# Stick-breaking attention: running products against differences of successive values, in place of a second sigmoid and a product per key

## The chip, the core and the metric

The kernel runs on one core of a Trainium2 chip. The metric is the device time of one execution in microseconds, the median of several. The engines are TensorE (PE, with its weight loads shown as PEld), VectorE (DVE), ScalarE (ACT), GpSimd (POOL) and SyncE (SP), which issues the DMAs of this kernel. Each engine works through its own instructions in order and waits on semaphores.

## What is computed

A decoder trunk of two layers over 1024 tokens of width 1024, in float32. The even layer has two kinds of softmax attention, the odd one stick-breaking attention with 16 heads of width 64; each is followed by a SwiGLU layer, and a norm closes. The change touches stick-breaking attention alone:

```python
z = jnp.einsum('bhqd,bhkd->bhqk', q_c, k).astype(jnp.float32) * scale
log_rest = jnp.where(strict, jax.nn.log_sigmoid(-z), 0.0)
suffix = lax.cumsum(log_rest, axis=3, reverse=True) - log_rest
a = jnp.where(strict, jnp.exp(jax.nn.log_sigmoid(z) + suffix), 0.0)
return jnp.einsum('bhqk,bhkd->bhqd', a.astype(v.dtype), v)
```

`strict` keeps the keys ahead of the query. With m the sigmoid of −z (1 where masked) and R(j) the product of m over the keys from j on, the weight of key j is (1 − m(j)) R(j+1), which is R(j+1) − R(j). A sum over keys of these differences times v(j) is therefore the sum of R(j) (v(j−1) − v(j)) plus the last value of the block, as R behind the last key is 1 and the value ahead of the first key counts as 0.

## The kernel before, in words

`sb_attention` works on eight chunks `i` of two heads `hh` each. A chunk's attention is cut into units `unit(i, hh, c)`, `c` from 0 to 3, each with two blocks of 128 query rows (`qb`) against `nk = (qb + 1) * 128` keys. A unit has three stages. `s0` loads the queries twice over the partitions (`qs`). `s1` makes the scores of both blocks on TensorE into one of two PSUM tiles (`b..s`, `ps_s`), two sigmoids on ScalarE (`m` of −z, `e` of z), a scan from the right on VectorE that turns `m` into running products, and a multiply on VectorE, of `e` by `m` shifted by one key, which gives the weights:

```python
nc.scalar.activation(like(m, sv, 0, nk), sv, AF.Sigmoid, scale=-1.0)
nc.scalar.activation(like(e, sv, 0, nk), sv, AF.Sigmoid)
...
nc.vector.tensor_tensor(e[:, :nk - 1], e[:, :nk - 1], m[:, 1:nk], op=ALU.mult)
```

`s2` turns the weights by transposes on TensorE into PSUM (`b..t`), splits them there into a rounded high half (`ph`, ScalarE) and the rest (`pl`, VectorE), and multiplies both by V, whose 128 columns hold the high and the low half of a head's 64 values (`b..o`, one PSUM tile, `ps_o`). ScalarE copies the lower 64 rows out and VectorE adds them to the upper ones (`ot`), and the result is stored to DRAM (`o2T_d`). TensorE can start the next unit's `b..o` only behind that sum.

The projections are generators that `run_segments` runs between the units as fill: `qk_chunk(i)` makes a chunk's queries and keys (`sqo`, `qc`, `kc`, `ks`) in 8 steps, `v_chunk(i)` makes V for two chunks (`svo`, `sv`) in 8 steps, one for each tile of 128 tokens. V of the first two chunks is made alone, ahead of any unit; V of chunks 2 and 3, 4 and 5, 6 and 7 beside the units of chunks 1, 3 and 5. In the last two chunks the fill is the output projection (`obo`), whose weights (`obw`) are loaded then.

The order on each engine is not written out by hand: a scheduler at build time lays the instructions out by its own estimate of when each can run, and each engine then keeps to that order.

Of the kernel before, what the change touches and what calls it, by code (L numbers as in the profile page):

```python
# [11 lines left out]
F32 = mybir.dt.float32  # L12
# [3 lines left out]
ALU = mybir.AluOpType  # L16
# [23 lines left out]
def trunk(ctx: ExitStack, tc: tile.TileContext, x, norm_mix, norm_ffn, norm_final,  # L40
# [19 lines left out]
    def ps_t(name):  # L60
        return ps.tile([128, 512], F32, name=name, tag="t", bufs=3)
# [86 lines left out]
    def alt(pf, i):  # L148
        return pf[i % len(pf)] if pf else None
# [908 lines left out]

    def sb_attention(h, op):
        w_in = odd_w_in[0]  # L1060
        with pool("sv", 2) as sv_, pool("sq", 2) as sq, pool("sa", 2) as sa:
            vbox, qbox = {}, {}

            def v_chunk(i, pf=None):
                w = load_w(w_in, 0, KT, [(2 * D + i * 256, 256)], f"sv{i}", nc.gpsimd)
                vs = [sv_.tile([128, NT, 2, 128], F32R, name=f"sv{i}{j}", tag="V", bufs=3) for j in range(2)]
                vbox[2 * i], vbox[2 * i + 1] = vs
                for tt in range(NT):
                    o = proj_tok(h, tt, w, 256, f"svo{i}{tt}", alt(pf, tt))
                    for j in range(2):  # L1070
                        src = o[:, j * 128:(j + 1) * 128].rearrange("p (h d) -> p h d", d=64)
                        nc.scalar.copy(vs[j][:, tt, :, 0:64], src)  # L1072
                        nc.vector.tensor_tensor(vs[j][:, tt, :, 64:128], src,  # L1073
                                                vs[j][:, tt, :, 0:64].bitcast(F32), op=ALU.subtract)
                    yield

            def qk_chunk(i, pf=None, by_half=False):
# [31 lines left out]
            def unit(i, hh, c):  # L1109
# [10 lines left out]
                def s1():  # L1120
                    qst = pts.pop()
                    kst = qbox[i][1][hh]
                    for qb in (2 * c, 2 * c + 1):
                        nk = (qb + 1) * 128
                        s = ps_s(f"{nm}s{qb}")
                        qsl = slice(qb % 2 * 128, (qb % 2 + 1) * 128)
                        sv = qk(s, (qst[:, 0, qsl], qst[:, 1, qsl]), kst, 0, nk, [(nk - 128, m_strict)])
                        e = sa.tile([128, (c + 1) * 256], F32, name=f"{nm}e{qb}", tag=f"E{c}", bufs=2)
                        m = sa.tile([128, (c + 1) * 256], F32, name=f"{nm}m{qb}", tag=f"M{c}", bufs=1)
                        nc.scalar.activation(like(m, sv, 0, nk), sv, AF.Sigmoid, scale=-1.0)  # L1130
                        nc.scalar.activation(like(e, sv, 0, nk), sv, AF.Sigmoid)
                        mr = m[:, :nk][:, ::-1]
                        nc.vector.tensor_tensor_scan(mr, mr, zc[:, :1].to_broadcast([128, nk]), 1.0,
                                                     op0=ALU.mult, op1=ALU.add)
                        nc.vector.tensor_tensor(e[:, :nk - 1], e[:, :nk - 1], m[:, 1:nk], op=ALU.mult)
                        pts.append(e)

                def s2():
                    v = vbox[i]
                    o = ps_o(f"{nm}o")[:, :256]  # L1140
# [28 lines left out]
                    nc.scalar.copy(tmp[0:64], o[64:128, :])  # L1169
                    nc.vector.tensor_tensor(tmp[pr], o[0:64, :], tmp[0:64], op=ALU.add)  # L1170
                    if i == 7:
# [14 lines left out]
            for i in range(8):  # L1186
# [3 lines left out]
                elif i % 2 == 1:  # L1190
                    segs.append((units, [v_chunk((i + 1) // 2), qk_chunk(i + 1)], 16, 2))
                elif i == 6:
# [77 lines left out]
```

## Time and profile before

| | |
|---|---|
| runs | 2796.96 us median of 3 (2796.86 to 2797.99) |
| profiled execution | 2809.49 us, span of its instructions 2807.7 us |
| busy share of the span | TensorE 95%, its weight loads 82%, VectorE 67%, ScalarE 44%, GpSimd 19% |
| stick-breaking layer | from about 1464 to 2110 us of the span |

The span goes from the first to the last instruction. A wait is idle time of an engine right ahead of an instruction, with the instruction of another engine that ended it. Names are those of the program: `b613o` is the output tile of unit i = 6, hh = 1, c = 3, and `<-` stands between what is written and what is read. The granted clock (PEclk) is 1.00 at TensorE's 2.4 GHz and 0.50 at 1.2 GHz. Shares of idle time in a stretch are its length less the engine's busy time.

### The profile page before, as it was taken

Reading aid. Unit: us, or ns where it says so; the run is one execution under the profiler, and the core shown is the slowest. Engines: PE = TensorE matmul, PEld = TensorE weight load, DVE = VectorE, ACT = ScalarE, POOL = GpSimd, SP = SyncE. Lnnn points to the kernel's source line nnn. Section 1 sums busy time; section 2 is a strip of 40 time slices with the busy share of each in tenths; the row PEclk is TensorE's granted clock in tenths of the full one; section 3 lists DMA queues with packets and bytes.
Section 4 is the critical chain, followed back from the end, with each engine's and each line's share of the span. In section 5 each row is a group of like instructions: output and inputs, shape, how many; then the busy total and the mean of one; then the engine's idle time right before and its main releaser. Section 6 shows DMA issues by size and latency. Waiting matters only on the chain.

```text
span 2807.7 us, 42453 instructions
## 1 busy us (share of the span) xinstructions
PE 2668.3 (95%) x15596; PEld 2307.8 (82%) x15596; DVE 1880.9 (67%) x3266; ACT 1244.9 (44%) x2603; POOL 525.6 (19%) x637
## 2 busy tenths in 40 slices
PE   8999999999979999999999999999887999999998
PEld 7889888898967888888887888787786788888887
DVE  7467667556586666657554767877848657665755
ACT  4366666544353333334443545554425333333433
POOL 3465655444120000000022020211102000000000
PEclk9999999999989999999999999999998999999999
DMA  5100000013445555577643233324434545556754
GB/s 157 32 23 7 23 21 22 23 45 95 123 175 176 150 163 166 159 224 240 198 162 87 59 83 69 94 68 110 124 102 166 174 153 167 160 158 212 256 186 141
DMA packets 327904, 347.70 MB, mean 124 GB/s; under 512 B 24560, under 2 KB 280208, under 8 KB 327696
## 3 DMA queue, kind: packets, MB, share of 16 engines
q1 hardware_dynamic: 327696, 344.98, 40.5%
q8 instruction: 124, 2.03, 0.3%
q14 instruction: 84, 0.69, 0.1%
HBM read 223.79 MB, written 95.94 MB: 114 GB/s over the span
## 4 chain that ended last, share of the span: by engine, by line
PE 69%; DVE 13%; DMA 9%; issue 4%; ACT 4%; POOL 2%; SPq 1%; DVEq 0%; POOLq 0%; ACTq 0%
PE f0o L128 2%; PE f0o L126 2%; PE f0o L127 2%; PE f1o L128 2%; PE f1o L126 2%; PE f1o L127 2%; PE sqo L126 2%; PE sqo L127 2%; PE sqo L128 2%; DMA f1t<-in_ffn_w_down_dram 1%; PE svo L126 1%; PE svo L128 1%; PE svo L127 1%; DMA t_d<-f1t 1%; PE oao L127 1%
## 5 line engine op out<-in xcount | busy, mean ns | idle before, releaser
L113 POOL TENSOR_SCALAR sv0h<-sv0r 128x1024 fp32r<-128x1024 f32 x2 | 2.1, 1057 | 598.9 <-DVE f0c L1043 595.2
L167 POOL TENSOR_TENSOR nf0r<-nf0v,mhalf 128x1 f32<-128x1 f32 x1 | 0.6, 553 | 600.6 <-DVE nf0v L165 600.6
L208 PEld LDWEIGHTS <-ident_b 128*128 128x128 bf16 x352 | 34.2, 97 | 48.2 <-issue 35.7
L1043 DVE TENSOR_TENSOR f1c<-f1o,f1c 128x512 f32<-128x512 f32 x56 | 36.0, 687 | 30.2 <-PE f1o L128 30.1
L1043 DVE TENSOR_TENSOR f0c<-f0o,f0c 128x512 f32<-128x512 f32 x56 | 36.0, 684 | 18.8 <-PE f0o L128 18.8
L951 DVE TENSOR_TENSOR f1t<-f1t 128x256 f32<-128x256 f32 x22 | 9.4, 425 | 51.0 <-DMA f1t<-in_ffn_w_down_dram 51.0
L951 DVE TENSOR_TENSOR f0t<-f0t 128x256 f32<-128x256 f32 x22 | 9.4, 425 | 50.2 <-DMA f0t<-in_ffn_w_down_dram 50.2
L1072 ACT CAST sv<-svo 128x128 fp32r<-128x128 f32 x64 | 17.0, 268 | 48.7 <-PE svo L128 36.3
L1073 DVE TENSOR_TENSOR sv<-svo,sv 128x128 fp32r<-128x128 f32 x64 | 18.2, 286 | 30.0 <-ACT sv L1072 29.8
L702 POOL TENSOR_SCALAR obh<-obr 128x1024 fp32r<-128x1024 f32 (+1 forms) x8 | 12.1, 1530 | 88.8 <-DMA obr<-o2T_d 45.0
L1102 DVE TENSOR_TENSOR kc<-sqo,kc 128x512 fp32r<-128x512 f32 x16 | 11.0, 689 | 23.4 <-ACT kc L1101 23.3
L735 DVE TENSOR_TENSOR xr<-obo,xr 128x256 f32<-128x256 f32 x32 | 13.3, 419 | 18.1 <-PE obo L128 17.9
L735 DVE TENSOR_TENSOR xr<-oao,xr 128x256 f32<-128x256 f32 x32 | 13.3, 419 | 16.6 <-PE oao L128 16.4
L1097 DVE SCALAR_TENSOR_TENSOR qc<-sqo,qc 128x512 fp32r<-128x512 f32 x16 | 11.0, 687 | 18.5 <-ACT qc L1096 18.5
L1101 ACT CAST kc<-sqo 128x512 fp32r<-128x512 f32 x16 | 9.4, 588 | 30.3 <-PE sqo L128 30.3
L126 PE MATMUL cgo<-cgh,hah 128*128 128x280 f32 x64 | 19.7, 309 | 1.7 <-ACT hah L192 1.7
L128 PE MATMUL cgo<-cgh,hal 128*128 128x280 f32 x64 | 20.0, 313 | 0.0
L127 PE MATMUL kso<-ksl,hah 128*128 128x256 f32 x64 | 18.9, 296 | 1.2 <-POOL ksl L115 1.2
L127 PE MATMUL cgo<-cgl,hah 128*128 128x280 f32 x64 | 19.5, 305 | 0.0
L126 PE MATMUL kso<-ksh,hah 128*128 128x256 f32 x64 | 18.6, 294 | 0.9 <-ACT gates L400 0.9
L126 PE MATMUL q0o<-q0h,hah 128*128 128x256 f32 x64 | 19.1, 301 | 0.0
L126 PE MATMUL dk1o<-dk1h,hah 128*128 128x256 f32 x64 | 18.8, 294 | 0.1
(9997 smaller groups left out, 11121.6 us busy)
## 6 DMA issues: line engine op xcount, KB each, us to landing
f0t<-in_ffn_w_down_dram SPq DMA_DIRECT2D x44, 256.0 KB, 3.9
t_d<-f0t SPq DMA_DIRECT2D x22, 512.0 KB, 3.0
f1t<-in_ffn_w_down_dram SPq DMA_DIRECT2D x44, 256.0 KB, 3.9
t_d<-f1t SPq DMA_DIRECT2D x22, 512.0 KB, 2.9
f0dr<-t_d SPq DMA_DIRECT2D x20, 512.0 KB, 4.9
f1dr<-t_d SPq DMA_DIRECT2D x20, 512.0 KB, 5.1
x_d<-xr SPq DMA_DIRECT2D x64, 128.0 KB, 2.3
ks<-kc SPq DMA_DIRECT2D x64, 128.0 KB, 2.3
```

Source lines behind the costliest of these rows:

```text
L126: nc.tensor.matmul(o, a[0], b[0], start=start, stop=False, skip_group_check=onto)
L127: nc.tensor.matmul(o, a[0], b[1], start=False, stop=False, skip_group_check=onto)
L128: nc.tensor.matmul(o, a[1], b[0], start=False, stop=stop, skip_group_check=onto)
L208: nc.tensor.matmul(s[:, b, mo:mo + 128], ident_b, m, start=False, stop=i == len(here) - 1)
L702: nc.gpsimd.tensor_scalar(hs, raw, 1.0, 1.0, op0=ALU.mult, op1=ALU.mult)
L735: nc.vector.tensor_tensor(xr, o[:, :256], xr, op=ALU.add)
L951: nc.vector.tensor_tensor(b11, b12, b11, op=ALU.subtract)
L1043: nc.vector.tensor_tensor(cv, o, cv, op=ALU.add)
L1072: nc.scalar.copy(vs[j][:, tt, :, 0:64], src)
L1073: nc.vector.tensor_tensor(vs[j][:, tt, :, 64:128], src, vs[j][:, tt, :, 0:64].bitcast(F32), op=ALU.subtract)
L1097: nc.vector.scalar_tensor_tensor(lo, o, SCALE, hi.bitcast(F32), op0=ALU.mult, op1=ALU.subtract)
L1102: nc.vector.tensor_tensor(kc[:, 1, :], o, kc[:, 0, :].bitcast(F32), op=ALU.subtract)
```

## The change

The second sigmoid and the multiply go, and with them the tiles `e`. The transposes read the running products, `m`, which now has two buffers (three for the larger `c`) in place of one. V holds differences: `v_chunk` copies a projected tile to SBUF (`vf`), shifts it by one token by DMAs (rows 0 to 126 into rows 1 to 127 of `d`, called `vb` in the pool; row 127 into row 0 of the next tile's), and subtracts; the split into high and low halves then reads the difference from SBUF in place of PSUM. Row 127 of each tile, the last value of each block of keys, also goes by DMA into a row of `rows`, which four small transposes turn into `ends`, and `s2` adds the right column of `ends` in the sum that makes `ot`. That makes a ninth step of `v_chunk`, and the fill count of its segments goes from 16 to 17.

```diff
             def v_chunk(i, pf=None):
...
                 vs = [sv_.tile([128, NT, 2, 128], F32R, name=f"sv{i}{j}", tag="V", bufs=3) for j in range(2)]
-                vbox[2 * i], vbox[2 * i + 1] = vs
-                for tt in range(NT):
-                    o = proj_tok(h, tt, w, 256, f"svo{i}{tt}", alt(pf, tt))
+                ends = sv_.tile([64, 4, NT], F32, name=f"se{i}", tag="ends", bufs=2)
+                rows = sv_.tile([NT, 256], F32, name=f"sr{i}", tag="rows", bufs=1)
+                vbox[2 * i], vbox[2 * i + 1] = [(vs[j], ends[:, 2 * j:2 * j + 2, :]) for j in range(2)]
+                before = [sv_.tile([128, 256], F32, name=f"sb{i}0", tag="vb", bufs=5)]
+                nc.vector.memset(before[0][0:1, :], 0.0)
+                steps = []
+
+                def split(tt):
+                    d, vf = steps[tt]
+                    nc.vector.tensor_tensor(d, d, vf, op=ALU.subtract)
                     for j in range(2):
-                        src = o[:, j * 128:(j + 1) * 128].rearrange("p (h d) -> p h d", d=64)
+                        src = d[:, j * 128:(j + 1) * 128].rearrange("p (h d) -> p h d", d=64)
                         nc.scalar.copy(vs[j][:, tt, :, 0:64], src)
                         nc.vector.tensor_tensor(vs[j][:, tt, :, 64:128], src,
                                                 vs[j][:, tt, :, 0:64].bitcast(F32), op=ALU.subtract)
+
+                for tt in range(NT):
+                    o = proj_tok(h, tt, w, 256, f"svo{i}{tt}", alt(pf, tt))
+                    vf = sv_.tile([128, 256], F32, name=f"sf{i}{tt}", tag="vf", bufs=4)
+                    nc.scalar.copy(vf, o[:, :256])
+                    d = before.pop()
+                    nc.sync.dma_start(d[1:128, :], vf[0:127, :])
+                    nc.sync.dma_start(rows[tt:tt + 1, :], vf[127:128, :])
+                    if tt < NT - 1:
+                        before.append(sv_.tile([128, 256], F32, name=f"sb{i}{tt + 1}", tag="vb", bufs=5))
+                        nc.sync.dma_start(before[0][0:1, :], vf[127:128, :])
+                    steps.append((d, vf))
+                    if tt > 1:
+                        split(tt - 2)
                     yield
+                split(NT - 2)
+                split(NT - 1)
+                t = ps_t(f"set{i}")
+                for j in range(4):
+                    nc.tensor.transpose(t[:64, j * NT:(j + 1) * NT], rows[:, j * 64:(j + 1) * 64], ident[:NT, :NT])
+                nc.scalar.copy(ends, t[:64, :4 * NT].rearrange("p (j t) -> p j t", j=4))
+                yield
...
-                        e = sa.tile([128, (c + 1) * 256], F32, name=f"{nm}e{qb}", tag=f"E{c}", bufs=2)
-                        m = sa.tile([128, (c + 1) * 256], F32, name=f"{nm}m{qb}", tag=f"M{c}", bufs=1)
+                        m = sa.tile([128, (c + 1) * 256], F32, name=f"{nm}m{qb}", tag=f"M{c}", bufs=3 if c > 1 else 2)
                         nc.scalar.activation(like(m, sv, 0, nk), sv, AF.Sigmoid, scale=-1.0)
-                        nc.scalar.activation(like(e, sv, 0, nk), sv, AF.Sigmoid)
                         mr = m[:, :nk][:, ::-1]
                         nc.vector.tensor_tensor_scan(mr, mr, zc[:, :1].to_broadcast([128, nk]), 1.0,
                                                      op0=ALU.mult, op1=ALU.add)
-                        nc.vector.tensor_tensor(e[:, :nk - 1], e[:, :nk - 1], m[:, 1:nk], op=ALU.mult)
-                        pts.append(e)
+                        pts.append(m)
...
-                    v = vbox[i]
+                    v, ends = vbox[i]
...
-                    nc.vector.tensor_tensor(tmp[pr], o[0:64, :], tmp[0:64], op=ALU.add)
+                    for k in range(2):
+                        cs = slice(k * 128, (k + 1) * 128)
+                        nc.vector.scalar_tensor_tensor(tmp[pr, cs], o[0:64, cs], ends[:, hh, 2 * c + k:2 * c + k + 1],
+                                                       tmp[0:64, cs], op0=ALU.add, op1=ALU.add)
...
-                    segs.append((units, [v_chunk((i + 1) // 2), qk_chunk(i + 1)], 16, 2))
+                    segs.append((units, [v_chunk((i + 1) // 2), qk_chunk(i + 1)], 17, 2))
```

The order on the engines moves with it. First VectorE where unit b013 is finished and the units of chunk 1 begin, before (L1133 is the scan, L1135 the multiply, L1156 makes `pl`, L1170 makes `ot`):

```order
L1133 SCALAR_TENSOR_TENSOR b102m_18217<-b102m_18217,zc 128x640
L1133 SCALAR_TENSOR_TENSOR b101m_18083<-b101m_18083,zc 128x512
L1135 TENSOR_TENSOR b102e_18216<-b102e_18216,b102m_18217 128x639
L1135 TENSOR_TENSOR b101e_18082<-b101e_18082,b101m_18083 128x511
L1156 TENSOR_TENSOR b013pl_18015<-b013t_18009,b013ph_18014 128x512
L1156 TENSOR_TENSOR b013pl_18028<-b013t_18022,b013ph_18027 128x512
L1133 SCALAR_TENSOR_TENSOR b102m_18229<-b102m_18229,zc 128x768
L1133 SCALAR_TENSOR_TENSOR b103m_18362<-b103m_18362,zc 128x896
L1170 TENSOR_TENSOR b012ot<-b012o,b012ot 64x256
L1135 TENSOR_TENSOR b102e_18228<-b102e_18228,b102m_18229 128x767
L1156 TENSOR_TENSOR b013pl_18041<-b013t_18035,b013ph_18040 128x512
```

and the same place of the changed kernel (L1161 is the scan, L1183 makes `pl`, L1199 makes `ot`; `se` is `ends`):

```order
L1161 SCALAR_TENSOR_TENSOR b101m_18097<-b101m_18097,zc 128x512
L1183 TENSOR_TENSOR b013pl_18032<-b013t_18026,b013ph_18031 128x512
L1183 TENSOR_TENSOR b013pl_18045<-b013t_18039,b013ph_18044 128x512
L1199 SCALAR_TENSOR_TENSOR b012ot<-b012o,se_17041,b012ot 64x128 x2
L1183 TENSOR_TENSOR b013pl_18058<-b013t_18052,b013ph_18057 128x512
L1161 SCALAR_TENSOR_TENSOR b102m_18244<-b102m_18244,zc 128x640
L1161 SCALAR_TENSOR_TENSOR b102m_18253<-b102m_18253,zc 128x768
```

The multiplies are gone from between, the sum `ot` of unit b012 is two instructions, and the scans of block b102 stand behind the first three `pl` of b013 instead of among them.

Second, VectorE a little later, where V of chunks 2 and 3 is made, in the changed kernel (`sb` is the shifted tile `d`, `sf` the copied one; L1078 is the new subtraction, L1082 the split's):

```order
L1078 TENSOR_TENSOR sb10_18135<-sb10_18135,sf10_18162 128x256
L1199 SCALAR_TENSOR_TENSOR b013ot_18078<-b013o_18025,se0_17041,b013ot_18078 64x128 x2
L1082 TENSOR_TENSOR sv10_18131<-sb10_18135,sv10_18131 128x2x64
L1082 TENSOR_TENSOR sv11_18132<-sb10_18135,sv11_18132 128x2x64
L1078 TENSOR_TENSOR sb11_18166<-sb11_18166,sf11_18193 128x256
L1199 SCALAR_TENSOR_TENSOR b100ot_18114<-b100o_18100,se0_17041,b100ot_18114 64x128 x2
L1082 TENSOR_TENSOR sv10_18131<-sb11_18166,sv10_18131 128x2x64
L1082 TENSOR_TENSOR sv11_18132<-sb11_18166,sv11_18132 128x2x64
L1183 TENSOR_TENSOR b101pl0_18263<-b101t0_18257,b101ph0_18262 128x512
L1183 TENSOR_TENSOR b101pl2_18275<-b101t2_18270,b101ph2_18274 128x256
```

Before, only the split's instructions (L1073), which read the projection's PSUM tile, stood in these places; now a subtraction that waits for a DMA stands directly ahead of `ot` of units b013 and b100 and ahead of `pl` of b101.

Third, TensorE behind the last matmul of that V, in the changed kernel (L205 and L208 make scores and add the mask, L1103 are the four transposes of `rows`, L1177 the transposes of a unit):

```order
L128 MATMUL svo17_18498<-sv1h4_18127,hcl11_16744 128x256
L205 MATMUL b112s4_18763<-ks11_17528,b112qs_18672 128x320 x4
L208 LDWEIGHTS ident_b_76
L208 MATMUL b112s4_18763<-m_strict_85,ident_b_76 128x128
L205 MATMUL b112s5_18772<-ks11_17528,b112qs_18672 128x384 x4
...
L205 MATMUL b113s6_18848<-ks11_17528,b113qs_18760 128x448 x4
...
L205 MATMUL b113s7_18857<-ks11_17528,b113qs_18760 128x512 x4
...
L1103 MATMUL set1_18542<-ident_69,sr1_18134 64x8 x4
L1177 MATMUL b103t0_18566<-ident_69,b103m6_18405 128x128
```

The transposes of `rows` are new there; four blocks of scores stand between them and the projection in this chunk, two in the next two chunks of V, and 31 projection matmuls in the first.

## Rows read from the trace of the kernel before

**Rows 1.** The page's first part: busy us (share of the span) xinstructions.

```profile
PE 2668.3 (95%) x15596; PEld 2307.8 (82%) x15596; DVE 1880.9 (67%) x3266; ACT 1244.9 (44%) x2603; POOL 525.6 (19%) x637
```

**Rows 2.** Busy time by stretch of the stick-breaking layer, whole core.

```profile
core 0: us, PE busy (x) PEld busy (x) DVE busy (x) ACT busy (x) POOL busy (x), PEclk, DMA share, GB/s
1520.00:1600.00 80.00, 70.20 (x422) 59.47 (x420) 68.38 (x87) 46.34 (x99) 9.22 (x4) 0.94 0.33 74
1600.00:1680.00 80.00, 77.10 (x488) 67.36 (x488) 52.63 (x74) 38.25 (x84) 15.64 (x9) 1.00 0.29 70
1680.00:1760.00 80.00, 75.72 (x528) 67.99 (x528) 64.53 (x96) 44.72 (x104) 14.46 (x8) 0.98 0.31 72
1760.00:1840.00 80.00, 76.48 (x444) 64.22 (x443) 61.34 (x81) 43.74 (x89) 14.56 (x8) 1.00 0.38 91
1840.00:1920.00 80.00, 76.55 (x513) 68.40 (x512) 58.16 (x83) 40.97 (x95) 11.37 (x7) 0.98 0.28 67
1920.00:2000.00 80.00, 70.90 (x440) 60.51 (x439) 71.54 (x93) 43.72 (x90) 13.54 (x9) 0.96 0.48 123
2000.00:2060.00 60.00, 52.70 (x395) 50.25 (x396) 48.46 (x67) 22.34 (x48) 8.37 (x6) 0.91 0.38 112
```

**Rows 3.** TensorE's waits from 1520 to 2060 us, longest first: total, times, longest.

```profile
PE b613o L1162 <- DVE b612ot L1170: 2.9, 1, 2.9
PE b602t L1150 <- DVE kc L1102: 2.7, 1, 2.7
PE b002o L1162 <- DVE b001ot L1170: 2.7, 1, 2.7
PE b213t L1150 <- DVE b212pl L1156: 1.7, 1, 1.7
```

**Rows 4.** Busy time right behind the wait of `b002o`; columns as in rows 2.

```profile
1540.10:1546.90 6.80, 5.96 (x25) 5.29 (x25) 6.28 (x12) 2.06 (x6) 0.00 (x0) 0.50 0.56 132
```

**Rows 5.** Busy time of line 1135, the multiply, in the whole layer.

```profile
1464.00:2130.00 666.00, 103.60 (x128) 0.97 0.37 96
```

**Rows 6.** Busy time of line 1131, the second sigmoid, whole layer.

```profile
1464.00:2130.00 666.00, 83.90 (x128) 0.97 0.37 96
```

**Rows 7.** Groups by line and shape: busy us, mean ns | idle before.

```profile
L1130 ACT ACTIVATE b113m<-b113s 128x1024 f32<-128x1024 f32 x1 | 1.0, 1028 | 2.4 <-DVE b113e L1135 2.4
L1133 DVE TENSOR_TENSOR_SCAN b013m<-b013m,zc 128x1024 f32<-128x1024 f32 x1 | 2.3, 2292 | 1.2 <-ACT b013m L1130 1.2
L1135 DVE TENSOR_TENSOR b013e<-b013e,b013m 128x1023 f32<-128x1023 f32 x1 | 1.2, 1225 | 0.1
L1073 DVE TENSOR_TENSOR sv<-svo,sv 128x128 fp32r<-128x128 f32 x64 | 18.2, 286 | 30.0 <-ACT sv L1072 29.8
L735 DVE TENSOR_TENSOR xr<-obo,xr 128x256 f32<-128x256 f32 x32 | 13.3, 419 | 18.1 <-PE obo L128 17.9
```

**Rows 8.** Tile `b102ot`: duration ns min/median/max, first and last start us.

```profile
L1169 ACT COPY b102ot<-b102o x1: 375/375/375, 1619.4 to 1619.4; 64x256 f32<-64x256 f32 x1
```

**Rows 9.** Groups of TensorE by line and shape, columns as in rows 7.

```profile
L1150 PE MATMUL b703t<-ident,b703e 128*128 128x128 f32 x15 | 2.3, 273 | 0.0
L205 PE MATMUL b103s<-ks,b103qs 128*128 128x512 f32 x4 | 1.2, 419 | 0.0
```

**Rows 10.** Line 1105, DMA issues: duration ns min/median/max, first, last start.

```profile
L1105 SPq DMA_DIRECT2D ks<-kc x64: 461/572/944, 1506.6 to 1978.9; - x64
```

**Rows 11.** ScalarE in order of time, V projected alone: start, us, instruction.

```profile
1483.79 0.27 ACT L1072 CAST sv<-svo 128x128 fp32r<-128x128 f32 x1 [1.99 <-PE svo L128]
1486.67 0.27 ACT L1072 CAST sv<-svo 128x128 fp32r<-128x128 f32 x1 [1.99 <-PE svo L128]
```

**Rows 12.** The page's sixth part: DMA issues, KB each, us to landing.

```profile
ks<-kc SPq DMA_DIRECT2D x64, 128.0 KB, 2.3
```

## Prediction

> **What bounds the kernel now.** I read the page's busy times first, then busy time by stretch, then TensorE's waits, then the groups of the two operations that go. The reader is to see in the first that TensorE is busy for 95% of the span and VectorE for 67% [rows 1]: work taken from VectorE counts only where TensorE waits for it. The change touches the stick-breaking layer alone, which runs from 1464 to about 2110 us of the span; ahead of it the order of every engine stays as it was, and in the second SwiGLU layer behind it the same work only changes places by some rows.
>
> In that layer the stretches [rows 2] show two things side by side. TensorE is idle for 80 − 70.20 = 9.80 us of the first 80 us, then 2.90, 4.28, 3.52, 3.45 and 9.10 us, and 7.30 us of the last 60: together 40.35 us. VectorE's share in the same stretches is 85, 66, 81, 77, 73, 89 and 81%. The two stretches with most idle time are those with the fullest VectorE; at 66 to 77% the idle time is 2.9 to 3.5 us. The waits say the same of single places [rows 3]: the long ones of TensorE end on VectorE, on the small sum of a unit's outputs (`ot`), on the low halves (`pl`), on the keys' low halves (`kc`). These are not the removed multiply itself, but instructions that stand behind it on VectorE's queue. The multiply sits in front of them 128 times.
>
> The third cost is the clock. The granted clock over these stretches is 0.94, 1.00, 0.98, 1.00, 0.98, 0.96 and 0.91 [rows 2]; with 0.06 × 80 + 0.02 × 80 + 0.02 × 80 + 0.04 × 80 + 0.09 × 60 that is 16.6 us lost. Right after the 2.7 us wait before `b002o` the clock stood at 0.50 (1.2 instead of 2.4 GHz) for a whole 6.8 us, in which TensorE was busy 5.96 us [rows 3, 4]. So at most 40 + 17 = 57 us can be won here, if nothing of TensorE's own work changes.
>
> **What goes.** 128 multiplies on VectorE, 103.60 us in sum, 0.81 us each [rows 5]; 128 sigmoids on ScalarE, 83.90 us, 0.66 us each [rows 6]. The path of a block shortens, too: for the last row block of a head, scores to transposes was sigmoid 1.03 us, a second sigmoid of the same width, scan 2.29, multiply 1.23 [rows 7]; the scan does not read the second sigmoid, so the path loses the multiply, 1.2 us, and, where ScalarE is behind, up to 1 us more. A score bank is free one sigmoid earlier. And the single buffer of `m` made ScalarE wait for the multiply of the block before (2.4 us ahead of `b113m` [rows 7]); with two or three buffers that wait goes.
>
> **What comes.** On VectorE: 32 subtractions of 128x256 at 0.42 us (a sum of that size [rows 7]) = 13.4 us; the 64 subtractions into the low half of V stay at 0.29 [rows 7], reading SBUF instead of PSUM; the unit's sum of 64x256 becomes two of 64x128, at 0.29 each by the row of that width, against 0.41: 64 × 0.17 = 11 us. Net on VectorE 104 − 24 = 80 us less, 15 points of its share over the 540 us. On ScalarE 32 copies of 0.38 us [rows 8] = 12 us against 84. ScalarE is busy for 37 to 58% of these stretches [rows 2] and stays hidden.
>
> On TensorE: 16 transposes of eight rows. The nearest row has 15 transposes in 2.3 us [rows 9]: 0.15 each, 2.5 us; bounds 0 and 2.5, I take 2.
>
> On SyncE: 23 more DMAs for each of four chunks, each about 0.57 us to issue [rows 10], 13 us a chunk. Three of them per token tile are 1.7 us against the 2.88 us that a tile's projection takes [rows 11], so the queue keeps up where the tiles come back to back. Behind them stand the loads of `qs`, issued a unit ahead, the stores of `o2T_d`, which the output projection reads much later, and the weights' loads.
>
> **The two new waits.** (a) The transposes of `rows` need the last tile's row 127: copy 0.38, issue of the shift 0.57, then 2.3 us to landing by the DMA of `ks` [rows 8, 10, 12], 3.2 us after the projection's last matmul. In chunk 0, 31 projection matmuls stand between, which hides it; in chunk 1 four blocks of scores; in chunks 2 and 3 only two, of four matmuls and about 1.2 us each [rows 9], 2.4 us. Everything on TensorE is queued behind. Bounds 0 and 3 × 3.2 = 10 us; I take 3 × 1 = 3 us. (b) VectorE's subtraction waits for the shifted rows, up to 3.2 us behind the copy, and in the new order it stands directly ahead of `ot` and `pl` of the running unit (second piece of the order). But the next tile's projection covers 2.88 us of it on TensorE [rows 11]. Bounds: 0, and 24 tiles × 3.2 = 77 us if nothing were covered; nearest is the uncovered 0.3 us, 24 × 0.3 = 7 us, of which some falls where VectorE has slack: I take 3. The eight tiles of chunk 0 run before any unit and delay nobody.
>
> **The sum.** What idle time is left I read off the same table: VectorE's shares fall by 15 points to about 70, 51, 66, 62, 58, 74 and 66%. A stretch of before with such a share had 2.90 us idle at 66%, 3.45 at 73%, and none below is shown, so I give 3.2, 2.9, 2.9, 2.9, 2.9, 3.5 and, for 60 us, 2.2: 20.5 us. That is 20 us less. Stretches with up to 3.5 us idle lost 0 to 1.6 us to the clock, 0.5 on average; seven of them lose 3.7 instead of 16.6. Of the 13 us between, 88% (5.96 of 6.8 [rows 4]) were on busy time, and I take 10. Total 30 us won, 2 + 3 + 3 = 8 lost: 22 us less. The profiled execution took 2809.49 us (span 2807.7), 12.5 above the median of the runs, 2796.96. So span 2785, and median 2797 − 22 = 2775 us.
>
> **Rivals.**
> *More comes back.* If nearly every wait on VectorE vanishes and the clock stays up, 57 − 8 = 49 us: 2748. For it: nearly all long waits of TensorE end on VectorE. Against it: the stretch with VectorE at 66% still had 2.90 us idle [rows 2].
> *Nothing comes back.* TensorE's order was laid out again for the shorter chain. If transposes now stand closer behind their scores, a wait returns with the same length, as the order gives away what the chain saved: idle stays at 40, the clock too, and 2 + 3 remain to be paid, so 2797 + 5 = 2802; with half of it, 2797 − 15 + 8 = 2790. The pieces of the order speak for it a little: fewer rows stand between a scan and what reads it. Against it: VectorE's load falls by 80 us whatever the order. The Trainium skill, "Perfetto Trace Analysis", section "Identifying the Most-Contended Engine", says to improve the engine with the highest occupancy first and to judge TensorE by its weight loads. By that TensorE is the engine (its loads fill 438 of the 540 us of the seven stretches), the change adds to it, and the time would be 2802 as well; the same page's next section says to go after what fills the gaps of that engine, which is the forecast's side. The trace has both: high occupancy and gaps that end on VectorE [rows 2, 3].
> *Slower.* The shifted rows come late. If VectorE stood for half of the 3.2 us at each of the 24 tiles of chunks 1 to 3 with TensorE waiting behind, 24 × 1.6 = 38 us, in place of the 3 taken: 2797 − 22 + 35 = 2810. It turns the gain into a loss from about 1.1 us per tile on. For it: an in-order VectorE, three DMAs in one in-order queue, copies on a ScalarE that itself waits for casts. Against it: 2.88 us of cover per tile, and the buffers (five and four) let copies run ahead.
>
> **Chances.** The likeliest case, gain of 10 to 42 us: 0.68. More: 0.08. Nothing or nearly nothing (2790 to 2802): 0.15. Slower by the rows: 0.09. A measurement of this kernel can tell 0.2%, 5.6 us, from no change: faster means below 2791.4, slower above 2802.6. From the cases: faster 0.68 + 0.08 + 0.05 = 0.81, same 0.10, slower 0.09. Leaving out a tenth on each side, the range is 2750 to 2797; the likeliest case alone spans 2755 to 2787.
>
> **What the profile of the changed kernel would show.** Right: VectorE's busy time in the seven stretches near 345 us instead of 425, TensorE in them idle for some 20 us with the clock at 0.98 or better, the layer ending some 20 us earlier, the copy of `ends` hardly waited for. Wrong: TensorE's waits as long as before but ending on scans or sigmoids (nothing comes back); waits of `ot`, `pl` or casts behind line 1078 that end on a DMA, or TensorE standing more than 3 us ahead of line 1103 (slower). Idle time well below 15 us would mean that 2.9 us was no floor, and the time lies under 2760.

## The result, and the profile after

The changed kernel takes 2944.65 us (median; 2933.94 to 2946.79) against 2797.47 us for the kernel before in the same measurement: ratio 1.0513, 95% interval 1.0482 to 1.0543. The forecast of 2775 us was a gain; the change is a loss, and the time lies 170 us above the forecast. The page's first part of the changed kernel, to be set beside [rows 1]:

```profile
span 2944.3 us, 42511 instructions
...
PE 2702.4 (92%) x15612; PEld 2337.5 (79%) x15612; DVE 1810.4 (61%) x3238; ACT 1183.9 (40%) x2511; POOL 514.6 (17%) x637
```

VectorE lost 70 us of work and ScalarE 61, as the change is meant to do. TensorE's share nevertheless fell from 95 to 92%: it waits. Where, a table by stretch shows. The stretches are cut where TensorE begins a stage: the lone projection of the first V; then alternately chunks of units beside which no V is made (2nd, 4th, 6th row) and chunks beside which it is (3rd, 5th, 7th); the last row is the rest of the layer's units. Changed kernel, columns as in [rows 2]:

```profile
1461.40:1548.90 87.50, 58.66 (x311) 51.48 (x309) 17.72 (x39) 12.00 (x36) 11.02 (x7) 0.79 0.19 52
1548.90:1595.40 46.50, 43.59 (x251) 35.89 (x251) 33.20 (x42) 21.75 (x45) 7.08 (x5) 1.00 0.40 91
1595.40:1720.50 125.10, 90.03 (x527) 79.72 (x526) 49.95 (x84) 34.10 (x85) 14.21 (x9) 0.81 0.25 58
1720.50:1772.20 51.70, 49.00 (x299) 41.30 (x298) 38.60 (x51) 24.46 (x54) 6.11 (x4) 1.00 0.39 91
1772.20:1895.10 122.90, 86.31 (x526) 76.33 (x524) 48.81 (x87) 33.77 (x86) 14.47 (x9) 0.83 0.24 57
1895.10:1946.90 51.80, 48.86 (x300) 41.25 (x298) 38.69 (x51) 24.40 (x54) 6.11 (x5) 1.00 0.39 91
1946.90:2072.10 125.20, 88.06 (x526) 77.77 (x524) 48.46 (x86) 33.71 (x86) 13.65 (x8) 0.84 0.22 52
2072.10:2237.70 165.60, 152.91 (x1081) 140.40 (x1079) 109.93 (x168) 56.59 (x124) 20.54 (x17) 0.96 0.46 126
sum 776.30, PE 617.43 PEld 544.14 DVE 385.37 ACT 240.78 POOL 93.17; mean PE 77.18 PEld 68.02 DVE 48.17 ACT 30.10 POOL 11.65
```

The same stages of the kernel before, cut in the same way:

```profile
1464.50:1511.10 46.60, 46.60 (x307) 42.87 (x306) 12.53 (x29) 10.20 (x27) 10.85 (x7) 1.00 0.27 74
1511.10:1565.50 54.40, 48.35 (x251) 39.75 (x251) 43.13 (x50) 30.68 (x60) 8.15 (x4) 0.91 0.36 83
1565.50:1652.80 87.30, 79.06 (x521) 69.88 (x520) 58.18 (x85) 39.75 (x92) 17.09 (x9) 0.98 0.28 68
...
1704.90:1785.20 80.30, 77.35 (x523) 69.38 (x521) 57.35 (x83) 41.24 (x94) 13.94 (x8) 0.98 0.32 77
...
1838.20:1918.40 80.20, 77.25 (x522) 69.28 (x520) 57.37 (x83) 41.19 (x94) 13.17 (x7) 0.98 0.30 71
...
sum 630.60, PE 581.11 PEld 514.00 DVE 453.11 ACT 300.33 POOL 103.10; mean PE 72.64 PEld 64.25 DVE 56.64 ACT 37.54 POOL 12.89
```

The four stages that make V grew by 40.9, 37.8, 42.6 and 45.0 us, 166 together. All others shrank, by 20.6 us together (776.30 − 630.60 = 145.7 in sum). The traced execution of the kernel before lay 12.5 us above its median, so the 20.6 us are rather too many. So the change does two things at once: the units are quicker, and the making of V is much slower. In the slow stages TensorE is idle for 29 to 37 us and the granted clock is 0.79 to 0.84 (a mean of its two levels, 1.00 and 0.50), so that its busy time grew too (90.03 for 79.06 us with nearly the same work, 527 matmuls for 521). Of the 166 us, 123.5 are idle time and 42.8 busy time.

TensorE's waits in the changed kernel, longest first, in the place of [rows 3]:

```profile
PE svo L126 <- ACT sf L1088: 33.2, 5, 8.1
PE sqo L126 <- ACT sf L1088: 13.7, 2, 7.4
PE set L1103 <- DMA sr<-sf: 11.0, 1, 11.0
PE set L1103 <- DMA sv3r<-in_odd_w_in_dram: 10.7, 1, 10.7
PE b502t L1177 <- ACT sf L1088: 6.9, 1, 6.9
PE b102t L1177 <- DVE sv L1082: 6.4, 1, 6.4
```

The longest no longer end on `ot`, `pl` or `kc`. Three of these six end on ScalarE's copy of a projected tile (`sf`, line 1088), and two stand ahead of the transposes of the end rows (`set`, line 1103). These transposes do not read `sv3r`, so the releaser named in the fourth line is probably not the true one. The groups by line, columns as in [rows 7], say what stands behind these waits:

```profile
L1078 DVE TENSOR_TENSOR sb<-sb,sf 128x256 f32<-128x256 f32 x32 | 15.0, 468 | 190.2 <-DMA sb<-sf 182.1
...
L1081 ACT CAST sv<-sb 128x128 fp32r<-128x128 f32 x64 | 16.3, 296 | 204.0 <-DVE sb L1078 204.0
...
L1103 PE MATMUL set<-ident,sr 8*64 8x8 f32 x16 | 1.4, 195 | 28.0 <-DMA sr<-sf 11.0
```

The new subtraction waits 182 us in all for the shifted rows, 5.7 us for each of 32; ScalarE's casts wait 204 us for the subtraction. One turn of this, in order of time, while V is projected alone:

```profile
1464.98 0.37 ACT L1088 COPY sf<-svo 128x256 f32<-128x256 f32 x1 [1.14 <-PE svo L128]
...
1465.38 0.78 SPq L1090 DMA_DIRECT2D sb<-sf  x1
...
1473.45 0.43 DVE L1078 TENSOR_TENSOR sb<-sb,sf 128x256 f32<-128x256 f32 x1 [6.25 <-DMA sb<-sf]
...
1473.91 0.50 ACT L1081 CAST sv<-sb 128x128 fp32r<-128x128 f32 x2 [7.43 <-DVE sb L1078]
...
1474.32 0.37 ACT L1088 COPY sf<-svo 128x256 f32<-128x256 f32 x1
...
1474.71 0.63 SPq L1090 DMA_DIRECT2D sb<-sf  x1
```

The shift is issued 0.40 us after the copy began; the subtraction starts 8.07 us later; the cast 0.46 behind that; and the *next* tile's copy 0.41 behind the cast, because it stands behind it on ScalarE. That is 9.34 us per tile, where [rows 11] have 2.88. During the transfer the DMA engines are nearly empty (columns as in [rows 2]; the last three are clock, DMA share and GB/s):

```profile
1467.80:1472.60 4.80, 4.80 (x43) 4.80 (x42) 0.00 (x0) 0.00 (x0) 0.00 (x0) 1.00 0.07 23
```

0.07 of 16 engines is about one engine, and 127 KB at 23 GB/s take 5.7 us. The theory to be tested is that the 127 rows go out through one DMA engine (A). Its rivals are the single-row transfers and SyncE's issue (B); the new subtraction's place in the order as such, whatever the transfer takes (C); and that the units' part gave nothing either (D). The scheduler at build time is called the planner from here on; it lays the order out anew for every edit, so for each run the order has to be looked at, too. Below, "behind the cast" counts the copies that stand on ScalarE behind a cast of the tile just before, of the 28 that have a tile before them; in the changed kernel it is 21.

### The profile page after: what moved, and what is told of

The parts are those of the page before. It is cut to its first block, busy times and chain, and to the rows that moved or that the text cites. A ratio compares the mean times of both kernels' runs of the same rounds, so it can differ in the third digit from the quotient of the medians.

```text
span 2944.3 us, 42511 instructions
## 1 busy us (share of the span) xinstructions
PE 2702.4 (92%) x15612; PEld 2337.5 (79%) x15612; DVE 1810.4 (61%) x3238; ACT 1183.9 (40%) x2511; POOL 514.6 (17%) x637
## 5 line engine op out<-in xcount | busy, mean ns | idle before, releaser
L1078 DVE TENSOR_TENSOR sb<-sb,sf 128x256 f32<-128x256 f32 x32 | 15.0, 468 | 190.2 <-DMA sb<-sf 182.1
L1081 ACT CAST sv<-sb 128x128 fp32r<-128x128 f32 x64 | 16.3, 296 | 204.0 <-DVE sb L1078 204.0
L208 PEld LDWEIGHTS <-ident_b 128*128 128x128 bf16 x352 | 34.2, 97 | 49.5 <-issue 37.4
L1043 DVE TENSOR_TENSOR f0c<-f0o,f0c 128x512 f32<-128x512 f32 x56 | 35.9, 682 | 18.8 <-PE f0o L128 18.8
L126 PE MATMUL svo<-sv0h,hch 128*128 128x256 f32 x64 | 20.3, 318 | 9.7 <-ACT sf L1088 9.7
L126 PE MATMUL svo<-sv3h,hch 128*128 128x256 f32 x64 | 20.5, 320 | 8.1 <-ACT sf L1088 8.1
L126 PE MATMUL svo<-sv2h,hch 128*128 128x256 f32 x64 | 20.2, 315 | 7.9 <-ACT sf L1088 7.9
L1103 PE MATMUL set<-ident,sr 8*64 8x8 f32 x16 | 1.4, 195 | 28.0 <-DMA sr<-sf 11.0
L126 PE MATMUL svo<-sv1h,hch 128*128 128x256 f32 x64 | 20.1, 315 | 7.5 <-ACT sf L1088 7.5
L1103 PEld LDWEIGHTS set<-ident,sr 8*64 8x64 f32 x16 | 1.1, 145 | 29.1 <-issue 29.1
L126 PEld LDWEIGHTS svo<-sv0h,hch 128*128 128x128 f32 x64 | 13.9, 218 | 10.2 <-ACT sf L1088 10.1
L126 PE MATMUL sqo<-hch,sqk00h 128*128 128x512 f32 x16 | 9.3, 579 | 13.7 <-ACT sf L1088 13.7
```

What stands on the lines that cost most here:

```text
L126: nc.tensor.matmul(o, a[0], b[0], start=start, stop=False, skip_group_check=onto)
L208: nc.tensor.matmul(s[:, b, mo:mo + 128], ident_b, m, start=False, stop=i == len(here) - 1)
L1043: nc.vector.tensor_tensor(cv, o, cv, op=ALU.add)
L1078: nc.vector.tensor_tensor(d, d, vf, op=ALU.subtract)
```

## The experiments

**The shift in two transfers.** 112 rows and 15 rows in the place of 127:

```diff
-nc.sync.dma_start(d[1:128, :], vf[0:127, :])
+nc.sync.dma_start(d[1:113, :], vf[0:112, :])
+nc.sync.dma_start(d[113:128, :], vf[112:127, :])
```

> The changed kernel with the shift of 127 rows issued as two DMAs, of 112 rows and of 15; nothing else. Theory A (the 127 rows all go through one of the 16 DMA engines, one packet after the other, so that they land 7 to 8 us after the issue instead of 2.3, and every engine stands behind it in order): 112 rows can be dealt out over 16 engines, the shift lands in 2.3 to 3 us, and the time is what was forecast, about 2775 us (2760 to 2800). Theory B (the rows of 1 KB that go in pieces of 64 bytes, and their long issue, block SyncE's queue): one DMA more per tile, so no better, 2940 to 2960. Theory C (any DMA there is too late, since the order puts the subtraction directly ahead of the units' work): over 2900.

Measured: 2805.05 us, ratio 1.0031 (1.0018 to 1.0044). One more DMA per tile, the same bytes, and 140 of the 147 us are gone. That is a point for A, though the time is 30 us above its 2775 and just outside its 2760 to 2800. The order moved with the edit: only 14 of 28 copies stand behind the cast, so this run alone does not separate the transfer from the order. TensorE's waits on the end rows remain:

```profile
PE set L1104 <- DMA sr<-sf: 4.9, 2, 2.5
...
PE b503t L1178 <- ACT se L1105: 3.1, 1, 3.1
```

**Cut at 122 rows.** The same edit with 122 and 5 rows.

> The same with 122 rows and 5: 122 is 2 times 61. The Trainium skill, page DMA: Bandwidth & Descriptors, section Why a DMA increments its semaphore by 16 and not by 1, says that the largest number up to 16 that divides the slowest dimension is the number of engines; by that two engines carry 61 rows each. Theory A: the transfer takes half as long as with one engine, some 2.7 us for its packets instead of 5.5 to 6, the landing falls to 4 to 5 us, and the time lies between the two, 2800 to 2880. Theories B and C: as with 127 rows, 2930 to 2960.

One run: 2839.74 us, between the two, as A has it. VectorE's wait for the shifted rows was 79.7 us in all, against 31.3 with 112 and 182.1 with 127 rows. On TensorE, VectorE, ScalarE and GpSimd every instruction stands in the same order as with 112 + 15 rows, so the 35 us between these two kernels are the transfers' alone. During a transfer of 122 rows (1463.5 to 1465.5 us of that trace) the DMA engines' share is 0.15 at 39 GB/s, about twice that of 127 rows.

**The units alone.** V is made as before the change, the units are those of the change (no second sigmoid, no multiply), and the end terms are zero.

> The attention half of the change alone: no second sigmoid, no multiply, the transposes read the running products, two or three buffers, the sum with the column of ends in two parts; V is made as before the change, and ends is set to zero, so that the values are not differences (that part of the computation is left out). No shift, no rows, no added transposes. The forecast's gain without its three costs was 30 us: 2765 (2750 to 2785). If the rival that nothing comes back holds, 2790 to 2800.

Measured: 2771.80 us, ratio 0.9910 (0.9893 to 0.9926). The removal is worth 25 us; D falls. The same eight stages in this kernel (the first three, and the sum):

```profile
1468.20:1514.80 46.60, 46.60 (x307) 42.83 (x306) 12.57 (x31) 10.10 (x27) 10.85 (x7) 1.00 0.28 74
1514.80:1561.20 46.40, 43.48 (x250) 35.85 (x248) 33.22 (x42) 21.72 (x45) 7.06 (x5) 1.00 0.40 91
1561.20:1641.10 79.90, 77.39 (x523) 69.66 (x522) 47.82 (x75) 31.52 (x76) 14.33 (x9) 0.98 0.32 77
...
sum 600.50, PE 569.83 PEld 506.00 DVE 373.87 ACT 231.25 POOL 90.44; mean PE 71.23 PEld 63.25 DVE 46.73 ACT 28.91 POOL 11.31
```

VectorE is 79 us lighter (453.11 − 373.87); TensorE's idle time in the eight stages falls from 630.60 − 581.11 = 49.5 to 30.7 us, and its busy time by 11.3 us, since the clock stays higher. These differences are between two traced executions and come to 30 us; the medians differ by 25.

**Without the single rows.** The transfer of 127 rows stays; the transfers of one row (row 127 to `rows`, and to row 0 of the next tile) are left out.

> The changed kernel with the shift of 127 rows as it is, but without the two DMAs of a single row for each tile: row 0 of each shifted tile and the tile of last rows are set to zero by VectorE instead (the first difference of each tile and the last values are left out). Theory A: the shift still goes through one engine, 2910 to 2945. Theory B: the blocked queue is free, most of the loss goes, below 2830.

One run: 2933.71 us. B falls for the bulk of the loss: at most some 11 us of 147.

**128 rows in one transfer.** The sharpest test of A: the shift itself differs by one row, and the transfer to row 0 that goes with it is one of those that the run before showed to matter little:

```diff
-nc.vector.memset(before[0][0:1, :], 0.0)
...
-nc.sync.dma_start(d[1:128, :], vf[0:127, :])
+nc.sync.dma_start(d[0:128, :], vf[0:128, :])
...
-nc.sync.dma_start(before[0][0:1, :], vf[127:128, :])
```

> The changed kernel with one transfer of 128 rows, unshifted (rows 0 to 127 to rows 0 to 127), in the place of the one of 127 rows, and without the transfer and the zeros of row 0: the differences are then of no use, but number, size and order of the work stay. It separates the row count from everything else of the shift. Theory A (127 rows go out on one DMA engine, 128 on sixteen): the transfer lands in 2 to 3 us and the time is 2785 to 2805. Theory C (it is the place of the subtraction in the order, or bytes, or the copy within SBUF as such): 2900 to 2945.

One run: 2796.37 us, 148 under the changed kernel, of which the 28 transfers to row 0 that are gone can be some of the 11 us of the run before. The shape that differs by one row lands in 2.0 us (page, DMA issues):

```profile
sb<-sf SPq DMA_DIRECT2D x32, 128.0 KB, 2.0
```

C falls: the subtraction stands where it stood, and is no trouble if the rows come at once. ScalarE's order is nearly that of the changed kernel, too (22 copies of 28 behind the cast, for 21), so here it is the transfer that makes the difference.

**The same 127 rows from another queue.** `nc.gpsimd.dma_start` for `nc.sync.dma_start` in that line.

> The changed kernel with the transfer of 127 rows issued from GpSimd's queue and not SyncE's, all else as it is. If the number of rows alone sets how many engines move them, it stays slow: 2900 to 2945. If that depends on the queue that splits the transfer, it lands quickly: 2790 to 2830.

One run: 2801.53 us, and the trace has

```profile
sb<-sf POOLq DMA_DIRECT2D x32, 127.0 KB, 2.2
```

So it is not the number of rows alone that makes the transfer slow, nor the shift by one row, which 112 rows have as well: it depends on the queue. That the queues split the rows differently over the engines is the explanation, not a thing measured here. The order moved in this run (12 of 28 behind the cast), so of the two numbers the landing, and not the time of the kernel, is the evidence.

**The remainder: SyncE's issue, the end rows, the casts.** With the quick shift (112 + 15) there were 33 us left between 2805 and the units' 2772. Four kernels were measured together (the kernel before in the same measurement: 2797.56 us):

> The shift in 112 + 15 rows, and the single-row transfers left out (zeros in their place: row 0 of each difference and the end rows are then wrong, which the timing does not need). It asks what the 33 us between the 112 + 15 version (2805 us) and the units alone (2772 us) are. Theory R (SyncE's issue: four transfers per tile fill its queue, and the shifts themselves land later behind them): 2780 to 2790. Theory W (ScalarE's casts and the transposes of the end rows wait in order, whatever the number of transfers): 2797 to 2805.

2795.25 us: between the two expectations, so it decides little, as leaving the rows out also takes the wait of the end rows' transposes away.

> The shift in 112 + 15 rows, and the 16 transposes of the end rows with their copy stand four steps later, behind the first two outputs of the next projection. Only the wait on the last row's landing and on the copy behind it is taken away (4.9 us and 6.6 us of TensorE's waits named in the 112 + 15 trace, 11 in all). If these are on the path: 2792 to 2798. Theory R: 2800 to 2806, since SyncE's queue stays as long.

```diff
-    t = ps_t(f"set{i}")
...
+    if (j, f) == (1, 0) and i % 2 == 0:
+        put_ends(i // 2)
```

(`put_ends` holds the four transposes and the copy, word for word; `qk_chunk` calls it ahead of its third output. The ninth step of `v_chunk` goes with it, and the fill count is 16 again.) 2785.18 us, ratio 0.9953 (0.9936 to 0.9969): 20 us under the 112 + 15 kernel, more than expected, and the waits of TensorE ahead of `set` and on the copy behind it are gone from the trace. The order of copies and casts is that of the 112 + 15 kernel. With SyncE's queue as long as before, theory R falls as an account of most of the remainder.

> The shift in 112 + 15 rows, and each tile's casts and second subtraction one tile later than its subtraction, so that ScalarE's cast finds the difference made (it waited 64.5 us for it in all, 32 times, in the 112 + 15 trace). Theory W: 2785 to 2797. Theory R: 2800 to 2806.

2801.96 us, ratio 1.0010 (0.9995 to 1.0025). This run tested nothing: the planner laid ScalarE out again, and copies and casts stand in the order of the kernel without the edit (14 of 28 behind the cast).

> Both of the two before: end rows late and casts late, on the 112 + 15 shift. Theory W: 2778 to 2790, faster than the kernel before. Theory R: 2797 to 2806.

2787.19 us, ratio 0.9956 (0.9939 to 0.9973): the end rows' part, and nothing more, for the same reason.

**Other queues for the single rows**, on the kernel with 112 + 15 rows and late end rows:

> The shift in 112 + 15 rows, end rows late, and the two single-row transfers of each tile issued from ScalarE's queue and not SyncE's, which has then two transfers per tile to issue. If SyncE's issue still holds the rest (the kernel without these transfers was 10 us quicker): 2776 to 2783. If ScalarE's own order pays for the 60 issues: 2785 to 2795.

> The same with the single-row transfers on GpSimd's queue, whose engine is nearly idle in this part. If SyncE's issue holds the rest: 2776 to 2783. If it doesn't, or if these transfers land much later by that queue: 2784 to 2795.

ScalarE's queue: 2780.58 us, ratio 0.9940 (0.9926 to 0.9955), inside the first expectation but not told apart from 0.9953; the order moved as well (4 of 28 behind the cast), so it does not show that SyncE's issue held anything. GpSimd's: 2794.08 us, ratio 0.9988 (0.9979 to 0.9998), slower than with SyncE; why, these runs do not settle.

**Late end rows on the slow shift.**

> The changed kernel with its one transfer of 127 rows, and only the transposes of the end rows four steps later. On the quick shift the same edit gave 20 us (2805 to 2785). If the two losses are independent: 2915 to 2930. If the slow transfers set the pace of the whole segment and the end rows wait inside that time: 2935 to 2948.

One run: 2932.23 us, between the two expectations. While the slow transfers hold everything up, little of the end rows' wait shows.

**The order on ScalarE.** The kernel is written with the split two tiles behind the copy, and with four and five buffers. ScalarE's order in the changed kernel, first V (`sf00` is the copied tile 0 of chunk 0, `sb00` its shifted tile, and so on), shows that the planner gave this up in most places:

```
1277 L1088 COPY sf00_17070<-svo00_17045 128x256
...
1279 L1081 CAST sv00_17039<-sb00_17043 128x2x64
1280 L1081 CAST sv01_17040<-sb00_17043 128x2x64
1281 L1088 COPY sf01_17101<-svo01_17076 128x256
...
1284 L1081 CAST sv00_17039<-sb01_17074 128x2x64
1285 L1081 CAST sv01_17040<-sb01_17074 128x2x64
```

Here each tile's cast stands ahead of the next tile's copy, so only one transfer is under way at a time. So it is for 21 of the 28 copies; where a copy does run ahead, as for tiles 4 and 6 of the first V, the subtractions follow at 5.6 and 5.7 us, elsewhere in this V at 9.1 to 9.5. Three kernels hold the written order (0 of 28 behind the cast):

```diff
-nc.vector.tensor_tensor(d, d, vf, op=ALU.subtract)
+tc.keep_in_program_order(nc.vector.tensor_tensor(d, d, vf, op=ALU.subtract))
...
-nc.scalar.copy(vs[j][:, tt, :, 0:64], src)
+tc.keep_in_program_order(nc.scalar.copy(vs[j][:, tt, :, 0:64], src))
```

> The changed kernel with its transfer of 127 rows, where the subtractions and ScalarE's casts are held in the order in which they are written: two tiles behind the copy, and not right behind their own tile's, where the planner puts them. Theory S (one loop per tile: copy, transfer of 6 us, subtraction, cast, next copy, so that the landing counts in full at each tile): with three tiles under way the pace falls from 9 us per tile to the 6 us that one transfer takes, and the time to 2830 to 2890. Theory E (the engine that moves the rows is the bound whatever the order): 2920 to 2945.

One run: 2869.20 us, 75 under the changed kernel with the transfer as slow as before. The subtractions now follow one another at the pace of the transfer:

```profile
1480.21 0.43 DVE L1078 TENSOR_TENSOR sb<-sb,sf 128x256 f32<-128x256 f32 x1 [3.66 <-DMA sb<-sf]
...
1485.88 0.42 DVE L1078 TENSOR_TENSOR sb<-sb,sf 128x256 f32<-128x256 f32 x1 [4.39 <-DMA sb<-sf]
...
1491.57 2.02 DVE L1078 TENSOR_TENSOR sb<-sb,sf 128x256 f32<-128x256 f32 x1 [4.02 <-DMA sb<-sf]
...
1497.18 0.43 DVE L1078 TENSOR_TENSOR sb<-sb,sf 128x256 f32<-128x256 f32 x1 [2.73 <-DMA sb<-sf]
```

5.7 us apart, and no longer 9.2. Theory S holds. What had been hidden comes out: TensorE now stands ahead of the end rows,

```profile
PE set L1103 <- DMA sr<-sf: 44.5, 4, 13.6
```

> 127 rows in one transfer, written order held, and end rows late. With order and end rows both mended, only the pace of one transfer after the other is left. Theory S: 10 to 25 us under the run with the written order alone. Theory E: within 10 us of 2932.

One run: 2830.87 us, 38 less, more than S gave it; late end rows are worth that much once the loop is broken.

> The shift in 112 + 15 rows, end rows late, subtractions and casts held in written order. In the earlier run with casts late the planner left ScalarE's order as it was, so that edit tested nothing; this one does. If the casts' waits for the subtraction (58.7 us on ScalarE with the end rows late) delay TensorE: 2772 to 2781. If they lie beside other work: 2782 to 2790.

2780.97 us, ratio 0.9922 (0.9905 to 0.9940), in the upper end of the first expectation. The interval touches that of the kernel without held order (0.9936 to 0.9969), so that step is small if it is there: with a quick transfer the order on ScalarE is worth little. Beside the changed kernel this version does the same sums in 164 us less, and it is 0.8% faster than the kernel before.

## Why the prediction was wrong

**The step that failed is the cost (b)**, the subtraction's wait for the shifted rows: taken at 3 us, bounds 0 and 77. It made up nearly all of the loss: 148 us went with a 128-row transfer in nearly the same order, 140 with the split shift. In the term's own measure, the four stages that make V grew by 166 us, 5.2 for each of 32 tiles, for the 3 us taken in all and an upper bound of 3.2 us per tile. Four choices in it were wrong.

*The landing time.* "3.2 us behind the copy" rests on 2.3 us to landing, from the 64-row transfer of the keys [rows 12]. The 127-row transfer needed 8.07 us from its issue to the subtraction. The row from the same queue and kind of memory was the wrong neighbour, since it differs in the row count. The upper bound of 77 us was built on the same 2.3 us and so was no bound.

*The cover.* "The next tile's projection covers 2.88 us of it" and "the buffers (five and four) let copies run ahead" suppose that copies do run ahead. ScalarE's order says otherwise: for 21 of 28 tiles the next copy stands behind the cast. The prediction looked at the new orders of VectorE and TensorE, and of ScalarE only at the load ("stays hidden"). It is ScalarE's order that closes the loop copy, transfer, subtraction, cast, copy. Nothing is covered in such a loop: 0.40 + 8.07 + 0.46 + 0.41 = 9.34 us per tile. With the slow transfer kept, breaking the loop gave back 75 us.

*The tiles of chunk 0.* "Run before any unit and delay nobody": they delayed TensorE itself, 46.6 to 87.5 us. Its projection waits for a PSUM tile that the copy has not emptied. Of the 28.8 us of idle time in this stage, 9.7 lie ahead of `svo` and 13.7 ahead of `sqo`, the queries and keys of chunk 0, both behind `sf`, and 5.4 ahead of `set`; the rest of the 33.2 us of `svo` belongs to the later V's.

*The clock.* The prediction gave the clock a price where waits go and none where new ones come. In the stages that make V, 42.8 of the 166 us are busy time, at a granted clock of 0.79 to 0.84.

The rival *Slower* named this mechanism and put it at 2810 us and a chance of 0.09; its price (1.6 us per tile, 24 tiles) came from the same landing time. The signs that it named came true: casts that wait behind line 1078 for a DMA, and TensorE standing 11.0 us ahead of line 1103.

**Cost (a)**, the transposes of the end rows: taken at 3 us, bounds 0 and 10. With the quick shift, putting them later gave 20 us, beyond the upper bound; with the slow one and held order 38 us, where TensorE had stood ahead of them for 44.5 us. Only 11 us of the 20 are named in the waits of the 112 + 15 kernel (4.9 on the landing, 6.6 on the copy behind it). The working counted the landing of the last row alone, not the copy of `ends` that the next unit's PSUM tile waits for; the rest, with what the fill count does, was not taken apart.

**What goes** was right in its mechanism and near in size. VectorE is 70.5 us lighter over the span, forecast 80. In the units alone TensorE's idle time falls by 49.5 − 30.7 = 18.8 us (forecast 20) and its busy time by 11.3 (forecast 10 from the clock), and the kernel gained 25 us, forecast 30; in the changed kernel itself the stages without V are 20.6 us shorter. *Nothing comes back* (2790 to 2802) and *More* (2748) are both excluded for the units alone: without the three costs they would be 2782 to 2797 and 2740 us, ratios of 0.995 to 1 and 0.980, outside the interval 0.9893 to 0.9926. The Trainium skill, "Perfetto Trace Analysis", section "Identifying the Most-Contended Engine", says to optimize the engine with the highest occupancy first. The prediction read from this, as a rival, that less work on VectorE would win nothing; the 25 us of the units alone side with the section behind it, on the gaps of the busiest engine.

**"The queue keeps up"** was right with a quick transfer and not with the slow one. SyncE's issue of a single-row DMA took 546 ns (median) with 112 + 15 rows, but in the changed kernel, where these stand behind the slow transfer:

```profile
L1091 SPq DMA_DIRECT2D sr<-sf x32: 530/1156/5203, 1466.2 to 2028.4; - x32
```

(duration ns min/median/max, first and last start). It is a consequence of the transfer rather than a cause: without the single-row DMAs the kernel was 11 us quicker at most.

**The account.** From the changed kernel on: held order −75 us (2869), late end rows −38 (2831), the shift in 112 + 15 rows −50 (2781), and 9 us lie between that and the units alone (2772). In another order the shares differ (the split first: −140, with part of the order's share in it, then end rows −20), because each delay hides part of the others. Several of these are single runs. Runs of one kernel lie up to 18 us apart (the kernel before, 2788.29 to 2806.05), and its medians in the five measurements are 2796.62 to 2802.81, so the steps are good to some 10 us. The last 9 us are less still: each against the kernel before of its own measurement, the two kernels are at 0.9922 and 0.9910, and the intervals overlap. With order, end rows and shift mended, what is left of the cost of the new V is thus 3 us by the ratios and 9 by the times, of the size of the 2 + 3 + 3 = 8 us that were forecast for it; these runs do not resolve it further.

## What to carry to other kernels

A transfer's time is to be taken from one of the same row count and the same queue, or bounded by one engine's pace: a shift by one row turns 128 rows into 127, and in this kernel, in the planner's order, that one row cost some 140 us of 2945. Where a DMA comes between two instructions of one in-order engine, look in that engine's final order for the loop that it closes, whatever the source's skew and buffers say, since a planner with other estimates may have undone them. And an edit that is meant to move an instruction has tested something only if the order on the engine shows that it moved; one that is not meant to may have moved it all the same.

## What the runs showed of the hardware

These are copies from SBUF to SBUF of rows of 1 KB, by row count and queue. 128 rows (unshifted) from SyncE's queue land in 2.0 us, 112 (shifted by one row) in 2.2, 127 (shifted) from GpSimd's queue in 2.2. 127 from SyncE's queue follow one another at 5.7 us, with 0.07 of the 16 DMA engines busy at 23 GB/s; with 122 rows it is 0.15 at 39 GB/s. The Trainium skill, "DMA: Bandwidth & Descriptors", section "Why a DMA increments its semaphore by 16 and not by 1", says that the number of engines is the largest one up to 16 that divides the slowest dimension on both sides (here the row count), with 127 rows as an example for one engine, and gives an exception on trn2 by which some direct copies from GpSimd's queue go out on all of them, 127 rows too. The landing times and the DMA shares above agree with it. By that rule 128 and 112 rows go out on sixteen engines and 122 on two; the DMA share with 122 rows, twice that with 127, agrees, and so does the time of the 122-row kernel between the other two (2839.74 us). A DMA of one row behind the slow transfer also held up SyncE, which issues it: the issue took up to 5.2 us in the changed kernel, against a median of 0.55 with 112 + 15 rows.
